# Linear attention: sixteen heads per load and store, Q in 8 KB runs, work still per eight heads

## The chip, the cores and the metric

One core of one Trainium2 chip. The metric is the device time of one execution in microseconds (us). Before: 127.53 us, the median of four runs (126.77 to 127.69). A run more than 1.5% above the fastest of its kernel is called slow and is left out of comparisons. A ratio is the mean time of one kernel's fast runs over that of the other kernel's fast runs of the same rounds, so it is not quite the ratio of the medians quoted; 95% intervals follow it in brackets.

## The reference, cut to what matters

```python
# Q, K, V: (8, 12, 512, 64) float32, so 96 heads of 512 rows
Q_feat = np.maximum(0, Q) + 1
K_feat = np.maximum(0, K) + 1
KV    = np.einsum('bhkd,bhkv->bhdv', K_feat, V)
K_sum = np.sum(K_feat, axis=2)
out   = einsum(Q_feat, KV) / (einsum(Q_feat, K_sum)[..., None] + 1e-10)
```

## The kernel before

Names first: DMA moves data between HBM and the core; DVE is the vector engine, ACT the scalar engine, PE the matrix engine, whose results land in the memory PSUM. A feature is the `max(0, x) + 1` of the reference. The work goes in twelve groups of eight heads. For each group DVE makes the features of K and Q. DVE (three blocks) and ACT (one block) copy V into a block-diagonal form, PE multiplies (`keys_values`), and ACT casts the result. PE transposes the Q features and ACT copies them out of PSUM (`transposes`). PE multiplies again and DVE divides (`output`). The functions that the argument touches, cut (`...` marks what is left out):

```python
def view(t, c):            # partition p holds c successive rows
    return t.flatten_outer_dims().rearrange("(n p c) d -> p n c d", p=P, c=c)
q_dram = view(Q, C2)       # C2 = 16 rows: runs of 4 KB of f32
...
def v_blocks(g):           # DVE takes blocks 0 to 2
    ...
        if b == 3:
            nc.scalar.copy(out=v_blk[g % 2][ps, b], in_=v_raw[ps])
...
def transposes(g):
    qf = qfs.pop(g)
    qt = mid_pool.tile([P, C, P, 2], BF16, name="qt")
    for half in range(2):
        qt_ps = psum_qt.tile([P, C, P], BF16, name="qt_ps")
        for c in range(C):
            nc.tensor.transpose(qt_ps[:, c, :], qf[:, half * C + c, :, :], identity)
        nc.scalar.copy(out=qt[:, :, :, half], in_=qt_ps)   # every 2nd element of qt
...
for g in range(NG - 1):
    k_features(g); v_blocks(g); q_features(g)
    if g:
        transposes(g - 1)
    if g >= 2:
        output(g - 2)
    keys_values(g)
    ...                    # loads and stores
```

## Time and profile before

| | before |
|---|---|
| median time, profiled span | 127.53, 125.8 us |
| ACT busy, of that in the 24 qt copies | 68.0, 29.7 us |
| DVE idle ahead of the output's reciprocals | 4.9 us |
| mean granted clock of PE | 0.839 |

### The profile page before, as it was taken

The numbers are of one execution on the slowest core, as the hardware profiler recorded it, in microseconds if no ns is written. First come the engines' busy times: TensorE is split into PE (matmuls) and PEld (weight loads), VectorE is DVE, ScalarE is ACT, GpSimd is POOL, SyncE is SP. The second block draws the span as 40 slices with busy tenths as digits, with TensorE's granted clock in tenths as the row PEclk, the third lists the DMA queues.
The fourth block names the chain that finished last, engine by engine and source line by source line (L and its number), as shares of the span: only waits on it lengthen the run. The fifth ranks groups of instructions, "written<-read, shape, count | busy, mean of one in ns | idle before, by whom it ended". The sixth has DMA issues, their size and how long they took to land.

```text
span 125.8 us, 2337 instructions
## 1 busy us (share of the span) xinstructions
PE 65.2 (52%) x960; PEld 48.4 (39%) x960; DVE 88.2 (70%) x188; ACT 68.0 (54%) x87; POOL 27.8 (22%) x43
## 2 busy tenths in 40 slices
PE   0005939000059784796918476006978569694500
PEld 0003627000036564574806365004656447472300
DVE  4896280206199799999989990629959999758920
ACT  7832296006700889629892962750087971987000
POOL 6990213000002082023700260212221002020000
PEclk9999999755555999689999999955589976999955
DMA  3999999999999999999999999999999999999991
GB/s 76 341 211 209 210 213 211 210 212 211 212 211 212 211 214 212 210 212 214 253 414 287 209 210 212 213 369 380 209 210 210 211 287 418 418 417 410 403 391 72
DMA packets 13419, 32.13 MB, mean 255 GB/s; under 512 B 608, under 2 KB 608, under 8 KB 13408
## 3 DMA queue, kind: packets, MB, share of 16 engines
q0 software_dynamic: 12048, 28.84, 98.3%
q1 hardware_dynamic: 1360, 3.15, 6.8%
q8 instruction: 7, 0.11, 0.3%
q14 instruction: 4, 0.03, 0.1%
HBM read 37.75 MB, written 12.58 MB: 400 GB/s over the span
## 4 chain that ended last, share of the span: by engine, by line
DMA 40%; DVE 26%; PE 18%; POOL 6%; issue 6%; DVEq 0%; POOLq 0%
DMA q_raw<-in_Q_dram 40%; DVE o_sb L200 15%; PE kva_ps L157 11%; DVE v_all L140 4%; PE qt_ps L176 3%; DVE recip L199 3%; PE o_ps L189 3%; POOL v_raw L99 2%; DVE qf L122 2%; DVE kf L122 2%; POOL q_raw L99 1%; POOL kva_diag L231 1%; POOL k_raw L99 1%; POOL identity masks.py:199 0%; POOL identity masks.py:197 0%
## 5 line engine op out<-in xcount | busy, mean ns | idle before, releaser
L157 PE MATMUL kva_ps<-v_all,kf 128*64 128x320 bf16 x384 | 36.4, 356 | 13.1 <-DVE v_all L140 13.1
L189 PE MATMUL o_ps<-kva_diag,qt 128*64 128x130 bf16 x384 | 19.1, 234 | 40.9 <-DVE o_sb L200 40.4
L200 DVE TENSOR_TENSOR o_sb<-o_ps,recip 128x512 f32<-128x512 f32 x48 | 33.2, 692 | 1.6
L140 DVE COPY v_all<-v_raw 32x2048 bf16<-32x2048 bf16 x36 | 26.5, 736 | 10.9 <-DMA v_raw<-in_V_dram 10.6
L157 PEld LDWEIGHTS <-kf 128*64 128x64 bf16 x384 | 25.3, 133 | 20.9 <-DVE v_all L140 13.3
L189 PEld LDWEIGHTS <-qt 128*64 128x64 bf16 x384 | 12.7, 114 | 46.4 <-DVE o_sb L200 44.6
L138 ACT COPY v_all<-v_raw 32x2048 bf16<-32x2048 bf16 x12 | 22.7, 1894 | 13.3 <-DMA v_raw<-in_V_dram 13.1
L177 ACT COPY qt<-qt_ps 128x1024 bf16<-128x1024 bf16 x24 | 29.7, 1308 | 0.3
L167 ACT CAST kva_diag<-kva_ps 64x256 bf16<-64x256 f32 x24 | 8.9, 371 | 33.3 <-PE kva_ps L157 33.2
L122 DVE TENSOR_SCALAR qf<-q_raw 128x1024 bf16<-128x1024 bf16 x24 | 9.1, 423 | 6.6 <-DMA q_raw<-in_Q_dram 6.5
L99 POOL DMA_DIRECT2D k_raw<-in_K_dram x7 | 5.3, 754 | 38.1 <-DVE kf L122 37.3
L116 POOL DMA_DIRECT2D out_dram<-o_sb x10 | 8.4, 846 | 22.6 <-DVE o_sb L200 16.4
L176 PE MATMUL qt_ps<-identity,qf 128*128 128x128 bf16 x192 | 13.1, 222 | 0.0
L199 DVE RECIPROCAL recip<-o_ps 128x8 f32<-128x8 f32 x48 | 9.6, 199 | 4.9 <-PE o_ps L189 4.8
L122 DVE TENSOR_SCALAR kf<-k_raw 128x1024 bf16<-128x1024 bf16 x22 | 8.7, 437 | 6.0 <-DMA k_raw<-in_K_dram 6.0
L176 PEld LDWEIGHTS <-qf 128*128 128x128 bf16 x192 | 11.0, 99 | 3.3 <-issue 3.0
L99 POOL DMA_DIRECT2D v_raw<-in_V_dram x8 | 6.1, 764 | 18.8 <-ACT v_all L138 10.7
L99 POOL DMA_DIRECT2D q_raw<-in_Q_dram x8 | 5.9, 741 | 4.2 <-DMA q_raw<-in_Q_dram 4.2
L213 DVE MEMSET v_all<- 128x3072 f32 (+1 forms) x2 | 4.4, 2192 | 1.1 <-DVE ones L225 0.7
L168 ACT CAST kva_diag<-kva_ps 64x4 bf16<-64x4 f32 x24 | 4.0, 169 | 0.0
L214 ACT COPY v_all<-zero 128x2048 f32<-128x2048 f32 x2 | 3.7, 1894 | 0.0
L214 ACT ACT_TABLE_LOAD x1 | 1.3, 1283 | 0.7 <-PEq L273 0.7
(12 smaller groups left out, 4.6 us busy)
## 6 DMA issues: line engine op xcount, KB each, us to landing
out_dram<-o_sb POOLq DMA_DIRECT2D x10, 1024.0 KB, 20.2
k_raw<-in_K_dram POOLq DMA_DIRECT2D x4, 1024.0 KB, 18.0
v_raw<-in_V_dram POOLq DMA_DIRECT2D x4, 1024.0 KB, 20.9
q_raw<-in_Q_dram POOLq DMA_DIRECT2D x4, 1024.0 KB, 25.0
v_raw<-in_V_dram POOLq DMA_DIRECT2D x4, 512.0 KB, 17.3
q_raw<-in_Q_dram POOLq DMA_DIRECT2D x4, 512.0 KB, 17.1
out_dram<-o_sb SPq DMA_DIRECT2D x4, 512.0 KB, 5.1
k_raw<-in_K_dram POOLq DMA_DIRECT2D x3, 512.0 KB, 23.3
```

The lines of the kernel that those rows point to most:

```text
L99: nc.gpsimd.dma_start(out=t[:, ms], in_=drams[x][:, 2 * groups[0] : 2 * groups[-1] + 2])
L116: nc.gpsimd.dma_start(out=o_to, in_=o_sb)
L122: nc.vector.tensor_scalar(out=dst, in0=src, scalar1=1.0, scalar2=1.0, op0=ALU.add, op1=ALU.max)
L138: nc.scalar.copy(out=v_blk[g % 2][ps, b], in_=v_raw[ps])
L140: nc.vector.tensor_copy(out=v_blk[g % 2][ps, b], in_=v_raw[ps])
L157: nc.tensor.matmul(kva_ps[64 * n : 64 * n + 64], lhsT=kf[:, c, n, :], rhs=vb[:, :, n, c, :], start=(c == 0), stop=(c == C2 - 1),)
L167: nc.scalar.copy(out=kva[ps, :, n, 0:D], in_=kva_ps[ps, sb : sb + 4, :])
L176: nc.tensor.transpose(qt_ps[:, c, :], qf[:, half * C + c, :, :], identity)
L177: nc.scalar.copy(out=qt[:, :, :, half], in_=qt_ps)
L189: nc.tensor.matmul(ops[c // 4][64 * j : 64 * j + 64, c // 2 % 2, (c % 2) * W : (c % 2) * W + W], lhsT=qt[:, c, 32 * b : 32 * b + 32, :], r ...
L199: nc.vector.reciprocal(out=recip, in_=cells[:, :, :, :, D:D1])
L200: nc.vector.tensor_tensor(out=o_sb[:, h:NP:2, 4 * i : 4 * i + 4].rearrange("p n (b c) d -> p b c n d", b=2), in0=cells[:, :, :, :, 0:D], i ...
```

## The change

Its intent is to move the same bytes in fewer and longer pieces: Q in runs of 8 KB, every bulk load and store 2 MB of f32. Work stays per eight heads, so the buffers for features and PSUM stay as they are. The core of the diff:

```diff
-    q_dram = view(Q, C2)
+    q_dram = view(Q, C4)          # C4 = 32 rows per partition: 8 KB runs
...
 def transposes(g):
-        qt = mid_pool.tile([P, C, P, 2], BF16, name="qt")
+        if g % 2 == 0:
+            qts[g // 2] = mid_pool.tile([P, C, P, 4], BF16, name="qt")
+        qt = qts[g // 2]
...
-            nc.scalar.copy(out=qt[:, :, :, half], in_=qt_ps)
+            nc.scalar.copy(out=qt[:, :, :, g % 2 * 2 + half], in_=qt_ps)
...
 def output(g):
-                        lhsT=qt[:, c, 32 * b : 32 * b + 32, :],
+                        lhsT=qt[:, c, q : q + 16, :],     # q = 16 * (4 * e + b)
...
 for g in range(last):
             if g:
                 transposes(g - 1)
+            if g % 2 == 0:
+                keys_values(g)
             if g >= 2:
                 output(g - 2)
-            keys_values(g)
+            if g % 2:
+                keys_values(g)
...
 # after the loop
-        transposes(last - 1)
         output(last - 2)
-        q_features(last)
         keys_values(last)
+        store(NS - 2)
+        q_features(last - 1)
+        transposes(last - 1)
+        q_features(last)
         transposes(last)
         output(last - 1)
         output(last)
```

One `qt` tile now serves both groups of a pair, and each head's columns come from four copies, two per group; what follows for the order of work is step 3 of the prediction. Not shown in the cut: output buffers fall from 6 to 3 (each of twice the size) and `qt` buffers from 3 to 2.

More of the change, by code (lines that the diff above doesn't have):

```diff
@@ L14 @@
 IN_BUFS = 2
-OUT_BUFS = 6
-LAG = 3
+OUT_BUFS = 3
 @with_exitstack
@@ L44 @@
     C2 = 2 * C
-    NPAIR = B * H * S // (P * C)
-    NP = 4
-    NG = NPAIR // NP
+    C4 = 4 * C
+    NS = B * H // 16
+    NG = 2 * NS
     D1 = D + 1
@@ L62 @@
     feat_pool = ctx.enter_context(tc.tile_pool(name="feat", bufs=2))
-    mid_pool = ctx.enter_context(tc.tile_pool(name="mid", bufs=3))
+    mid_pool = ctx.enter_context(tc.tile_pool(name="mid", bufs=2))
     out_pool = ctx.enter_context(tc.tile_pool(name="out_pool", bufs=OUT_BUFS))
@@ L76 @@
     kva_diag = [const.tile([P, 4, 2, D1], BF16, name=f"kva_diag{i}") for i in range(NV)]
-    drams = dict(k=k_dram, v=v_dram, q=q_dram)
     raw = {}
@@ L83 @@
     outs = {}
-    def own(g):
-        return slice(g % 2 * 2, g % 2 * 2 + 2)
-    def load_first_k():
-        k_raw = head_pool.tile([P, 2, C2, D], FP32, name="k_first")
-        nc.sync.dma_start(out=k_raw, in_=k_dram[:, 0:2])
-        raw["k", 0] = k_raw
-    def load(s, groups, names="kvq"):
-        ms = slice(groups[0] % 2 * 2, groups[-1] % 2 * 2 + 2)
-        for x in names:
-            if (x, "buf", s) not in raw:
-                raw[x, "buf", s] = in_pool.tile([P, 4, C2, D], BF16, name=f"{x}_raw")
-            t = raw[x, "buf", s]
-            nc.gpsimd.dma_start(
-                out=t[:, ms], in_=drams[x][:, 2 * groups[0] : 2 * groups[-1] + 2]
-            )
-            for g in groups:
-                raw[x, g] = t[:, own(g)]
@@ L105, in load_pair, with load_k @@
-    def load_pair(s):
-        if s < NG // 2 - 1:
-            load(s, (2 * s, 2 * s + 1))
-        else:
-            load(s, (2 * s,))
-            load(s, (2 * s + 1,))
-    def store(g):
-        o_sb = outs.pop(g)
-        o_to = o_dram[:, g * NP : g * NP + NP]
-        if g < NG - 2:
-            nc.gpsimd.dma_start(out=o_to, in_=o_sb)
-            return
-        for h in range(2):
-            nc.sync.dma_start(out=o_to[:, h:NP:2], in_=o_sb[:, h:NP:2])
+    def load_k(s, es=(0, 1)):
+        if s == 0 and es == (0,):
+            k_raw = head_pool.tile([P, 2, C2, D], FP32, name="k_first")
+            nc.sync.dma_start(out=k_raw, in_=k_dram[:, 0:4:2])
+            raw["k", 0] = k_raw
+            return
+        k_raw = in_pool.tile([P, 4, C2, D], BF16, name="k_raw")
+        lo, step = es[0], 3 - len(es)
+        nc.gpsimd.dma_start(
+            out=k_raw[:, lo:4:step], in_=k_dram[:, 4 * s + lo : 4 * s + 4 : step]
+        )
+        for e in es:
+            raw["k", 2 * s + e] = k_raw[:, e:4:2]
@@ new lines, in load_v, with load_q @@
+    def load_v(s):
+        v_raw = in_pool.tile([P, 4, C2, D], BF16, name="v_raw")
+        nc.gpsimd.dma_start(out=v_raw, in_=v_dram[:, 4 * s : 4 * s + 4])
+        for e in range(2):
+            raw["v", 2 * s + e] = v_raw[:, e:4:2]
+    def load_q(s):
+        q_raw = in_pool.tile([P, 2, C4, D], BF16, name="q_raw")
+        halves = [slice(e * C2, e * C2 + C2) for e in range(2)]
+        for cs in halves if s == NS - 1 else [slice(0, C4)]:
+            nc.gpsimd.dma_start(out=q_raw[:, :, cs], in_=q_dram[:, 2 * s : 2 * s + 2, cs])
+        for e in range(2):
+            raw["q", 2 * s + e] = q_raw[:, :, halves[e]]
@@ L121, in feature, with store @@
+    def store(s):
+        o_sb = outs.pop(s)
+        o_to = o_dram[:, 8 * s : 8 * s + 8]
+        if s < NS - 1:
+            nc.gpsimd.dma_start(out=o_to, in_=o_sb)
+        else:
+            for i in range(4):
+                nc.sync.dma_start(out=o_to[:, i:8:4], in_=o_sb[:, i:8:4])
     def feature(dst, src):
@@ L176, in transposes @@
                 nc.tensor.transpose(qt_ps[:, c, :], qf[:, half * C + c, :, :], identity)
-            nc.scalar.copy(out=qt[:, :, :, half], in_=qt_ps)
-        qts[g] = qt
+            nc.scalar.copy(out=qt[:, :, :, g % 2 * 2 + half], in_=qt_ps)
     def output(g):
+        s, e = g // 2, g % 2
         kva = kva_diag[g % NV]
-        qt = qts.pop(g)
-        o_sb = out_pool.tile([P, NP, C, D], FP32, name="o_sb")
+        qt = qts[s]
+        if e == 0:
+            outs[s] = out_pool.tile([P, 8, C, D], FP32, name="o_sb")
+        o_sb = outs[s]
         for h in range(2):
@@ L188, in output @@
                     b = 2 * h + j
+                    q = 16 * (4 * e + b)
                     nc.tensor.matmul(
                         ops[c // 4][64 * j : 64 * j + 64, c // 2 % 2, (c % 2) * W : (c % 2) * W + W],
-                        lhsT=qt[:, c, 32 * b : 32 * b + 32, :],
+                        lhsT=qt[:, c, q : q + 16, :],
                         rhs=kva[:, b],
@@ L200, in output @@
                 nc.vector.tensor_tensor(
-                    out=o_sb[:, h:NP:2, 4 * i : 4 * i + 4].rearrange(
+                    out=o_sb[:, 2 * e + h : 8 : 4, 4 * i : 4 * i + 4].rearrange(
                         "p n (b c) d -> p b c n d", b=2
@@ L207, in output @@
                 )
-        outs[g] = o_sb
     def clear(first, split, end):
@@ L219 @@
         nc.gpsimd.memset(zero, 0.0)
-        load_first_k()
-        load(0, (0,), "vq")
-        load(0, (1,))
+        load_k(0, (0,))
+        load_v(0)
+        load_q(0)
+        load_k(0, (1,))
         nc.vector.memset(ones, 0.0)
@@ L231 @@
             nc.gpsimd.memset(t, 0.0)
-        load_pair(1)
+        load_k(1)
+        load_v(1)
+        load_q(1)
         clear(5, 7, 9)
-        for g in range(NG - 1):
+        last = NG - 1
+        for g in range(last):
             k_features(g)
             v_blocks(g)
-            q_features(g)
+            if g < last - 1:
+                q_features(g)
             if g:
                 transposes(g - 1)
+            if g % 2 == 0:
+                keys_values(g)
             if g >= 2:
                 output(g - 2)
-            keys_values(g)
-            if g % 2 and g // 2 + 2 < NG // 2:
-                load_pair(g // 2 + 2)
-            if g >= LAG:
-                store(g - LAG)
-        last = NG - 1
+            if g % 2:
+                keys_values(g)
+                s = g // 2
+                if s + 2 < NS:
+                    load_k(s + 2)
+                    load_v(s + 2)
+                    load_q(s + 2)
+            elif g >= 4:
+                store(g // 2 - 2)
         k_features(last)
         v_blocks(last)
+        output(last - 2)
+        keys_values(last)
+        store(NS - 2)
+        q_features(last - 1)
         transposes(last - 1)
-        output(last - 2)
         q_features(last)
-        keys_values(last)
         transposes(last)
@@ L256 @@
         output(last)
-        for g in range(last - LAG, NG):
-            store(g)
+        store(NS - 1)
 _INS = ['Q', 'K', 'V']
```

## The prediction

> **What bounds the kernel now.** I read the page's shares first, then the slices and queues, then the chain of waits, then the timeline of the last 30 us.
>
> ```profile
> span 125.8 us, 2337 instructions
> ...
> PE 65.2 (52%) x960; PEld 48.4 (39%) x960; DVE 88.2 (70%) x188; ACT 68.0 (54%) x87; POOL 27.8 (22%) x43
> ...
> DVE  4896280206199799999989990629959999758920
> ...
> DMA  3999999999999999999999999999999999999991
> ...
> q0 software_dynamic: 12048, 28.84, 98.3%
> ```
>
> No compute engine is full; the DMA row is at 9 in every slice but the first and last. Loads are cast to bf16, so the page's GB/s count half of what they read. Counting HBM bytes, 37.75 MB read and 12.58 MB written are 50.3 MB. The trace's packets give the pace: loads of 4096 B of f32 run 412 per 4 us over 16 engines, one per 155 ns and engine, 422 GB/s; stores of 4096 B take 157 ns. 50.3 MB at 422 GB/s is 119.3 us of the 125.8. The rest is about 3 us ahead of the first data and 3 us at the ends.
>
> The landing events agree: in mid-kernel each 1 MB bf16 load (2 MB of f32) lands 5.0 us after its predecessor (39.1, 44.1, 49.0, 53.9, 58.9, 63.9), and the last four stores of 512 KB land at 121.1, 122.4, 123.6 and 124.9: a queue that is still draining.
>
> ```profile
> 8.65 25.48 DMA q_raw<-in_Q_dram
> ...
> 59.53 24.54 DMA q_raw<-in_Q_dram
> ```
>
> The chain of waits says it too: its two longest pieces are Q transfers. But between them it runs through DVE and PE, and in the last 40 us DVE is almost full. Compute is a close second. The timeline of the tail:
>
> ```profile
> 99.59 0.76 DVE L122 TENSOR_SCALAR qf<-q_raw 128x1024 bf16<-128x1024 bf16 x2
> ...
> 106.66 0.17 ACT L168 CAST kva_diag<-kva_ps 64x4 bf16<-64x4 f32 x1
> 106.84 0.38 ACT L167 CAST kva_diag<-kva_ps 64x256 bf16<-64x256 f32 x1
> 107.12 0.17 ACT L168 CAST kva_diag<-kva_ps 64x4 bf16<-64x4 f32 x1
> ...
> 107.31 1.89 ACT L138 COPY v_all<-v_raw 32x2048 bf16<-32x2048 bf16 x1
> ...
> 109.23 2.51 ACT L177 COPY qt<-qt_ps 128x1024 bf16<-128x1024 bf16 x2
> ...
> 109.77 2.07 PEld L157 LDWEIGHTS <-kf 128*64 128x64 bf16 x32
> 109.82 2.34 PE L157 MATMUL kva_ps<-v_all,kf 128*64 128x320 bf16 x32
> ...
> 113.55 0.21 DVE L199 RECIPROCAL recip<-o_ps 128x8 f32<-128x8 f32 x1 [1.69 <-PE o_ps L189]
> 113.79 0.69 DVE L200 TENSOR_TENSOR o_sb<-o_ps,recip 128x512 f32<-128x512 f32 x1
> ...
> 115.35 5.41 SPq L119 DMA_DIRECT2D out_dram<-o_sb  x4
> ```
>
> Two things to see. ACT serves in program order: the V copy at 107.31 has had its data since 102.3, but stands behind the kva casts, and those behind keys_values. And output(10) starts at 113.55 although qt(11) is copied only at 113.12 to 115.6: it needs qt(10) alone.
>
> **What the skill says.** "TensorE: Matmul & The Clock Gate", architectural detail: ACT and DVE are strict FIFO. The trace agrees (the V copy, 5 us late). Same page, Part 1: the PE clock is halved when idle and released after about 3.4 us of activity. It agrees: keys_values takes 2.3 us mostly, 3.6 to 4.5 in five of twelve groups. "DMA: Bandwidth & Descriptors", Why small descriptors are slow: about 3 cycles of overhead per packet. It is hardly visible here: stores in 2048 B packets go at 78 ns (512 KB per 1.25 us), so two make 156 ns against 155 for one of 4096 B. Same page, Rules: at least 1 MiB per DMA; the kernel before already has that.
>
> **The change, part by part.**
>
> 1. *Q in 8 KB runs.* 3072 Q packets become 1536 plus the split last load. At 1 ns (above) to 5 ns (the skill's three cycles, rounded up as an estimate) saved for each of some 90 packets per engine: 0.1 to 0.45 us.
>
> 2. *Fewer, larger DMAs.* The queue was never dry, so nothing is gained. Bytes and their order stay: before the last load both kernels place 4 MB of stores. The last load still lands near 104.5.
>
> 3. *The layout's price.* With 32 rows per partition, half of each partition's rows go to the even group and half to the odd. One head's rows thus come from both groups' transposes, and output(even) waits for qt of the odd group too. The order of instructions confirms it: the output of group 10 stands behind all four ACT copies of qt.
>
> For an even group the path is now: out(odd) begins at X on DVE; its last PE tile is written at X+2.0 (two tiles freed at 0.84 us each, 0.4 of matmuls); keys_values(odd) 2.3, X+4.3; four kva casts 0.9, X+5.2; ACT's V copy for the even group 1.9, X+7.1; two qt copies 2.5, X+9.6 (keys_values(even), 2.4 beside them, ends at X+9.5); first tile 0.3: out(even) at X+9.9 to 10.0. DVE meanwhile has 3.2 (output) + 0.8 + 2.3 + 0.8 (K, V, Q) = 7.1, so it idles 2.9 us per sixteen heads. Period: 10 + 3.2 + 3.9 = 17.0 us, against DMA's 15 us of loads, 20 with a 2 MB store.
>
> With landings as before, out(0) starts at 35.9 (PE's slow keys_values(2) from 31.4 to 35.5), out(1) at 42.9, then 59.9, 76.9, 93.9 for the odd ones. Before: 43.0, 57.3, 71.9, 93.4. So DVE falls 5 us behind by group 5 and the wait for Q at 84.1 gives it all back: the middle is nearly free, and the last loads are issued (73.9 to 77) before the queue is dry (about 87).
>
> 4. *The tail.* From X = 93.9: output(7) done 97.1. K (97.9), V lands about 99.2, V blocks 101.4, qt(9) copied 103.6, keys_values(10) 103.8, output(8) 104.0 to 107.2. K and V of 11: 110.3; output(9) to 113.5; Q features 10 and 11 only then, to 115.0. PE: last tile of output(9) 112.3, keys_values(11) 114.7, transposes(10) 115.7. ACT: kva casts to 115.6, then four qt copies at 1.25 = 5.0 (the transposes of 11 fit between them), 120.6. Output(10) begins at 121.0 where before it was 113.8. It and output(11) take 6.5: 127.5 (before 120.4).
>
> The DMA queue is empty by then: stores of 4 and 5, 6 and 7 end near 114, store of 8 and 9 is issued at 113.5 and lands near 122. So the last 512 KB only pays its own latency: the first K load of 1 MB took 5.0 us from issue to landing, less 1.25 for half the bytes is 3.7. Landing 131.2, and 0.9 to the end as before (124.9 to 125.8): span 132.1.
>
> Measured time exceeds the profiled span by 1.75 (127.55 less 125.8): 133.9. Minus 0.4 for Q, plus about 1 for PE's slow clock (1.7 us longer keys_values, weight about a third on two of them on the tail's path): 134.5.
>
> **Rivals.** (a) *DMA still sets the end*: 125.8 less 0.1 to 0.45 of packets, time about 127.2. For it: DMA at 9 everywhere and 2 MB transfers. Against: 120.6 for qt(11) rests on durations that hardly vary (ACT copies 1291 to 1332 ns) and on a fixed order. (b) *8 KB runs are really faster*, for instance 5% on Q (30 us): 126. Against: loads pace at 422 GB/s and show next to no cost per packet. Even then compute would end late. (c) *PE runs slow in most groups*: keys_values(odd) at 4 us adds 1.7 to each period of 17.0 and to both keys_values of the tail: 137 to 139. For it: five slow groups before, gaps of 4 us in PE's new order. Against: from 57 to 77 us it stayed fast with similar gaps. (d) *The tail's idle is smaller*, because DVE is earlier than I have it (V of the last load on time, ACT not blocked): 130 to 131.
>
> **Range and chances.** 134.5, with (d) at 130.5 and (c) at 138.5 as the ends. Faster by over 2% would need (b) and no tail: 0.04. Within 2% is (a), if my reading of the dependency in the tail is wrong somewhere: 0.12. Slower: 0.84.
>
> **What would show it.** Right: a new wait of PE's output, or its weight load, for ACT's qt of about 6 us ahead of output(10), the chain of waits ending in ACT qt and DVE o_sb; DVE idle about 3 us in front of each even output; DMA slices below 9 in the last 15 us; output(11) ending near 127; Q packets of 4096 B (bf16) at twice the old 155 ns pace within 3%; the middle's landings unchanged to 0.5 us. Wrong: DMA slices full to the end with a span under 127 (a or b), Q packets well below 300 ns, or output(10) starting before 117.

## More of the kernel before

From the page of the kernel before come the clock that PE was granted in 40 slices (tenths of full speed) and two groups of instructions. A group's line gives the count, then busy us and mean ns of one, then the idle time of the engine just before them and what ended most of it.

```profile
PEclk9999999755555999689999999955589976999955
...
L177 ACT COPY qt<-qt_ps 128x1024 bf16<-128x1024 bf16 x24 | 29.7, 1308 | 0.3
...
L199 DVE RECIPROCAL recip<-o_ps 128x8 f32<-128x8 f32 x48 | 9.6, 199 | 4.9 <-PE o_ps L189 4.8
```

A qt copy takes 1.3 us. The reciprocal is the first instruction of an output on DVE, so the idle time ahead of it is what outputs cost DVE in waiting: 4.9 us in the whole kernel. The 5s in the clock row are stretches in which PE ran at half speed.

## The result, and the profile after

| | before | after |
|---|---|---|
| median time | 127.53 (126.77 to 127.69) | 156.06 (155.68 to 156.75) |
| profiled span | 125.8 | 154.3 |
| ACT busy, of that qt copies | 68.0, 29.7 | 93.9, 56.5 |
| one qt copy | 1308 ns | 2494 ns |
| mean granted clock of PE | 0.839 | 0.784 |

Four runs of each. The ratio is 1.2257 [1.2186, 1.2328]: 22.6% slower, far beyond the range on record. From the page of the kernel after, the shares, slices, main queue and groups that answer to those shown before:

```profile
span 154.3 us, 2316 instructions
...
PE 81.6 (53%) x960; PEld 60.5 (39%) x960; DVE 89.0 (58%) x188; ACT 93.9 (61%) x87; POOL 21.8 (14%) x34
...
ACT  8413397499840996924996709969179800599000
...
PEclk9999996857955968768995879969599755995555
DMA  5999999999999999999999999999185000770085
...
q0 software_dynamic: 10624, 28.84, 80.3%
...
L178 ACT COPY qt<-qt_ps 128x1024 bf16<-128x1024 bf16 x24 | 56.5, 2494 | 4.9 <-PE qt_ps L177 4.7
L156 PE MATMUL kva_ps<-v_all,kf 128*64 128x320 bf16 x384 | 42.0, 394 | 27.8 <-DVE v_all L139 20.1
...
L203 DVE RECIPROCAL recip<-o_ps 128x8 f32<-128x8 f32 x48 | 9.6, 199 | 41.4 <-PE o_ps L193 41.4
```

First, DVE has hardly more work than before (89.0 against 88.2 us), but now waits 41.4 us ahead of its outputs. Second, ACT has gained 26 us of work, all of it in the qt copies: same shape, same count, nearly twice the time. Third, the DMA row is full for three quarters of the span and then falls to 0: the queue runs dry in the tail. Fourth, PE's clock is lower: the means of 0.784 and 0.839, with half speed and full speed as the only two levels in these traces, amount to 67 us at half speed against 40. A rival can be struck out here: no wait in this trace is put down to a store's landing or a `qt` buffer still in use, so the fewer buffers are not the cause.

The chain of waits of the kernel after shows one round of the loop (columns: start us, duration us, then engine, tile, line and count):

```profile
65.67 0.69 DVE o_sb L204
66.50 0.70 DVE o_sb L204
67.25 0.65 PE o_ps L193 x8
67.90 3.52 PE kva_ps L156 x32
72.36 1.89 ACT v_all L137
74.27 4.73 ACT qt L178 x2
79.75 0.69 DVE o_sb L204
...
86.81 0.69 DVE o_sb L204
```

This is the very loop of the prediction's step 3: the odd output's last tiles, `keys_values(5)`, ACT's casts and V copy, two qt copies, then the even output, and the next odd output at 86.8. Set beside the prediction's terms:

| term, us | predicted | measured |
|---|---|---|
| odd output's start to the last PE tile written | 2.0 | 2.4 |
| keys_values(odd) | 2.3 | 3.5 |
| kva casts | 0.9 | 0.9 |
| V copy | 1.9 | 1.9 |
| two qt copies | 2.5 | 4.7 |
| even output's first tile | 0.3 | 0.5 |
| DVE: even output, K, V, Q | 7.1 | 7.1 |
| period | 17.0 | 21.1 |

The column is the difference of successive starts in the chain and the trace, from 65.5 to 86.6. Every term has the place that was foreseen. Two of them are far off: the copies (+2.2) and `keys_values` (+1.2). The tail repeats it. From the same view:

```profile
129.44 3.47 PE kva_ps L156 x32
133.85 6.95 ACT qt L178 x3
140.81 2.27 ACTq L298
143.12 0.66 PE o_ps L193 x8
144.05 0.69 DVE o_sb L204
```

The step that the chain calls "ACTq 2.27" is the fourth qt copy. The timeline shows it as one row of four copies, 133.85 to 143.06. The prediction had this wait ("four qt copies at 1.25 = 5.0"). It lasts 9.2 us.

### The profile page after: what moved, and what is told of

The parts are those of the page before. It is cut to its first block, busy times and chain, and to the rows that moved or that the text cites. A ratio compares the mean times of both kernels' runs of the same rounds, so it can differ in the third digit from the quotient of the medians.

```text
span 154.3 us, 2316 instructions
## 1 busy us (share of the span) xinstructions
PE 81.6 (53%) x960; PEld 60.5 (39%) x960; DVE 89.0 (58%) x188; ACT 93.9 (61%) x87; POOL 21.8 (14%) x34
## 4 chain that ended last, share of the span: by engine, by line
DVE 32%; ACT 28%; PE 15%; DMA 15%; POOL 3%; issue 3%; ACTq 1%; POOLq 0%
ACT qt L178 20%; DVE o_sb L204 17%; DMA v_raw<-in_V_dram 15%; PE kva_ps L156 11%; DVE v_all L139 7%; ACT v_all L137 6%; PE o_ps L193 4%; DVE recip L203 4%; DVE kf L121 2%; DVE qf L121 2%; ACT kva_diag L166 2%; ACTq L298 1%; POOL kva_diag L235 1%; POOL k_raw L91 1%; ACT kva_diag L167 1%
## 5 line engine op out<-in xcount | busy, mean ns | idle before, releaser
L178 ACT COPY qt<-qt_ps 128x1024 bf16<-128x1024 bf16 x24 | 56.5, 2494 | 4.9 <-PE qt_ps L177 4.7
L156 PE MATMUL kva_ps<-v_all,kf 128*64 128x320 bf16 x384 | 42.0, 394 | 27.8 <-DVE v_all L139 20.1
L156 PEld LDWEIGHTS <-kf 128*64 128x64 bf16 x384 | 30.0, 147 | 36.6 <-DVE v_all L139 20.5
L193 PE MATMUL o_ps<-kva_diag,qt 128*64 128x130 bf16 x384 | 24.7, 279 | 36.2 <-DVE o_sb L204 24.6
L193 PEld LDWEIGHTS <-qt 128*64 128x64 bf16 x384 | 16.4, 140 | 45.0 <-DVE o_sb L204 30.5
L203 DVE RECIPROCAL recip<-o_ps 128x8 f32<-128x8 f32 x48 | 9.6, 199 | 41.4 <-PE o_ps L193 41.4
L177 PE MATMUL qt_ps<-identity,qf 128*128 128x128 bf16 x192 | 17.0, 258 | 4.1 <-ACT qt L178 4.1
L177 PEld LDWEIGHTS <-qf 128*128 128x128 bf16 x192 | 14.5, 118 | 7.3 <-issue 7.2
L91 POOL DMA_DIRECT2D k_raw<-in_K_dram x6 | 4.5, 754 | 56.5 <-DVE kf L121 56.5
L115 POOL DMA_DIRECT2D out_dram<-o_sb x5 | 5.6, 1115 | 45.4 <-DVE o_sb L204 45.4
L99 POOL DMA_DIRECT2D v_raw<-in_V_dram x6 | 4.6, 768 | 7.4 <-issue 3.9
L107 POOL DMA_DIRECT2D q_raw<-in_Q_dram x7 | 4.9, 709 | 0.0
```

The lines of the kernel that those rows point to most:

```text
L91: nc.gpsimd.dma_start(out=k_raw[:, lo:4:step], in_=k_dram[:, 4 * s + lo : 4 * s + 4 : step])
L115: nc.gpsimd.dma_start(out=o_to, in_=o_sb)
L156: nc.tensor.matmul(kva_ps[64 * n : 64 * n + 64], lhsT=kf[:, c, n, :], rhs=vb[:, :, n, c, :], start=(c == 0), stop=(c == C2 - 1),)
L178: nc.scalar.copy(out=qt[:, :, :, g % 2 * 2 + half], in_=qt_ps)
L193: nc.tensor.matmul(ops[c // 4][64 * j : 64 * j + 64, c // 2 % 2, (c % 2) * W : (c % 2) * W + W], lhsT=qt[:, c, q : q + 16, :], rhs=kva[:, ...
L203: nc.vector.reciprocal(out=recip, in_=cells[:, :, :, :, D:D1])
```

## The experiments

The first theory was that the slow copies are the cause, because they now write 8 bytes apart. Its rival was that PE's clock is: with longer waits PE is granted half its clock more often, `keys_values` gets longer, and the copies lie beside other work. A third thought was that the tail alone could be mended. Runs marked "wrong" compute a wrong result to isolate a cost; all others were correct.

**Copies with a step of 4 bytes, in the order of the kernel after** (wrong: neighbouring rows instead of interleaved ones).

```diff
-            qts[g // 2] = mid_pool.tile([P, C, P, 4], BF16, name="qt")
+            qts[g // 2] = mid_pool.tile([P, C, 2, P, 2], BF16, name="qt")
...
-            nc.scalar.copy(out=qt[:, :, :, g % 2 * 2 + half], in_=qt_ps)
+            nc.scalar.copy(out=qt[:, :, g % 2, :, half], in_=qt_ps)
```

> The changed kernel with one thing undone: the ACT copies of qt write every second bf16 (a step of 4 bytes, as in the kernel before) instead of every fourth (8 bytes); which half of a tile the output matmuls read is then wrong, so the result is wrong on purpose, but counts, sizes, order and the wait of output(even) for both groups' qt are kept. Theory (the copy's write step is the cause): copies fall from 2494 to about 1308 ns and the time to my own blind sum, 132 to 138 us. Rival (the order of instructions, the later stores and PE's slow clock are the cause): copies may fall, the time stays above 148 us.

Measured: 145.93 us (145.58 to 148.79, five runs), ratio 1.1427 [1.1358, 1.1495]. The clock row, `keys_values` and the qt group on its page:

```profile
PEclk9999995955985777965859955999857996589555
...
L156 PE MATMUL kva_ps<-v_all,kf 128*64 128x320 bf16 x384 | 46.4, 425 | 28.0 <-DVE v_all L139 20.6
...
L178 ACT COPY qt<-qt_ps 128x1024 bf16<-128x1024 bf16 x24 | 29.6, 1314 | 1.5 <-PE qt_ps L177 1.3
```

The copies are back at 1.31 us, so the write step is what slows them. They are worth 10.1 us (156.06 to 145.93). But 11.4 us remain above the 134.5 of the prediction (the blind sum from here on), where the copies' theory alone wanted nearly none: the time lies between the two expectations. The rest fits the clock rival: in this trace `keys_values` takes 4.0 to 4.5 us in ten of twelve groups, and in the chain two even ones (4.0 us each) now end later than the two copies beside them (2.5).

**Copies with a step of 8 bytes in the kernel before** (wrong).

```diff
-        qt = mid_pool.tile([P, C, P, 2], BF16, name="qt")
+        qt = mid_pool.tile([P, C, P, 4], BF16, name="qt")
...
-                        lhsT=qt[:, c, 32 * b : 32 * b + 32, :],
+                        lhsT=qt[:, c, 64 * (b // 2) : 64 * (b // 2) + 64, b % 2],
```

> The kernel before with only this added: qt has four slots per column, of which the ACT copies fill two, so they write with a step of 8 bytes; the output's weights are read with the same step (wrong result on purpose). Theory: copies rise from 1308 to about 2490 ns with everything else as it was, ACT's busy time from 68 to about 96 us, and the time to 129 to 137 us, since in this order an output waits only for copies of a group earlier. Rival (something else in the changed kernel makes its copies slow, such as PE's writes or waits beside them): copies stay near 1308 ns and the time within 1% of before.

Measured: 128.75 us (128.56 to 128.98, four runs), ratio 1.0094 [1.0054, 1.0135]. From its page:

```profile
DMA  3999999999999999999999999999999999999954
...
L177 ACT COPY qt<-qt_ps 128x1024 bf16<-128x1024 bf16 x24 | 56.9, 2505 | 0.3
```

The copies double here as well, in the old order and with nothing else changed but the step at which the output's weights are read. But the time hardly moves: just under the range expected. The same 27 us of ACT work cost 1.2 us where DMA stays at 9, and about 10 where the copies stand in the loop. So what counts is where the copies stand, not how busy ACT is.

**The cost of the step by itself** (wrong on purpose; one look): the kernel before with the steps 1, 2, 3, 4, 6 and 8 in successive groups (and 4 output buffers instead of 6).

```diff
+STEPS = (1, 2, 3, 4, 6, 8, 1, 2, 3, 4, 6, 8)
...
+            qt = qt[:, 0 : C * P * st].rearrange("d (c p k) -> d c p k", k=st, p=P)
```

> A measurement, in the kernel before: the twelve groups' qt copies write with steps of 1, 2, 3, 4, 6, 8, 1, 2, 3, 4, 6, 8 elements of bf16 (wrong result on purpose). Step 2 should give 1.31 us and step 4 2.49. If the cost follows the bytes spanned, step 1 gives about 1.05 (ACT's floor), step 3 about 1.9, step 6 3.7, step 8 4.9. If it is a step from one level to another, 6 and 8 give 2.5 as 4 does. If the skill's 16-byte lines (two hits per line at full rate) held for these writes, steps up to 4 would cost the same and 6 and 8 more.

| step, bf16 elements (bytes) | one copy of 1024 elements per partition, ns |
|---|---|
| 1 (2) | 1015 |
| 2 (4) | 1292 to 1319 |
| 3 (6) | 1866 to 1936 |
| 4 (8) | 2422 to 2578 |
| 6 (12) | 3617 to 3797 |
| 8 (16) | 4761 to 5062 |

From step 2 on the time goes in proportion to the step, about 0.6 ns per element and unit of step (2500 / 1024 / 4); at step 1 it stops at a floor of 1015 ns. The run took 142.3 us, against 127.5 for the kernel before on the same chip.

**The tail in another order**: the Q features and transposes of the last two groups ahead of their K and V work.

```diff
+        q_features(last - 1)
+        transposes(last - 1)
+        q_features(last)
+        transposes(last)
         k_features(last)
         v_blocks(last)
         output(last - 2)
         keys_values(last)
         store(NS - 2)
-        q_features(last - 1)
-        transposes(last - 1)
-        q_features(last)
-        transposes(last)
```

> The changed kernel, correct, its copies left slow, only the tail reordered: Q features and transposes of groups 10 and 11 go ahead of K, V and output(9). Theory (slow copies in every pair of groups, and four of them exposed in the tail): only the tail's part comes back, 156 to 147 to 151 us. Rival (the tail's order is most of the loss): 140 us or less.

Measured: 154.93 us (154.34 to 155.67, four runs), ratio 1.2149 [1.2086, 1.2211]: about 1 us better, if at all (its interval overlaps that of the kernel after), and a miss. Its timeline says why:

```profile
126.38 9.27 ACT L178 COPY qt<-qt_ps 128x1024 bf16<-128x1024 bf16 x4 [4.76 <-PE qt_ps L177]
...
135.67 1.89 ACT L137 COPY v_all<-v_raw 32x2048 bf16<-32x2048 bf16 x1
137.62 4.48 PE L156 MATMUL kva_ps<-v_all,kf 128*64 128x320 bf16 x32 [2.38 <-ACT v_all L137]
...
142.57 0.21 DVE L203 RECIPROCAL recip<-o_ps 128x8 f32<-128x8 f32 x1 [6.35 <-PE o_ps L193]
```

The four copies now run 7.5 us earlier, but ACT's V copy of group 11 stands behind them. `keys_values(11)` waits for that, at half clock, and the next output starts only 1.2 us earlier than before (142.8 against 144.0). The wait has changed its name.

**Filling PE's idle time**, to test the clock: 24 spare matmuls ahead of the second half of odd outputs and 14 ahead of even `keys_values`, into unused PSUM.

```diff
+    def fill(g, n):
+        ...
+        for _ in range(n):
+            nc.tensor.matmul(t, lhsT=identity, rhs=identity, start=True, stop=True)
...
+                fill(g, 14)
                 keys_values(g)
...
-                output(g - 2)
+                output(g - 2, 24 if g % 2 else 0)
```

With the 4-byte step (wrong, as its base):

> The kernel with copies at a step of 4 bytes (wrong result on purpose, 145.9 us) and, added, filler matmuls of 128 columns that nothing reads: 24 in the idle time of PE before the second half of each odd output, 14 before each even keys_values, so that PE's clock is not halved. Theory (what is left over my blind sum is PE's slow clock in both keys_values of a pair): keys_values falls from 4.0 to 2.3 to 2.7 us and the time to 134 to 139. Rival (the order of the waits, with PE's clock a bystander): keys_values falls and the time stays above 143.

Measured: 141.15 us (139.68 to 143.01, four runs); the two fast runs, 139.68 and 140.28, give 1.0996 [1.0927, 1.1065]. From its page:

```profile
L165 PE MATMUL kva_ps<-v_all,kf 128*64 128x320 bf16 x384 | 38.0, 367 | 18.6 <-DVE v_all L139 14.2
```

`keys_values` is busy for 38.0 us instead of 46.4, and the mean granted clock is 0.878 where the same kernel without fillers had 0.787. More work on PE makes the kernel some 6 us shorter: that part goes with the clock. Of the 5.5 us that remain above 134.5, some may be clock still: after the first 40 us its record has half speed from 63 to 67, 80 to 84, 111 to 121 us and from 128 to the end, the last two in the tail. The rest this run doesn't explain.

With the slow copies, in the kernel after itself (here 20 and 14 fillers, and 18 more ahead of even outputs):

> The changed kernel, correct, copies left slow at 2.5 us, with the same filler matmuls (20, 14, and 18 more between the even keys_values and the even output). If the two causes simply add, keys_values at 2.3 us takes 1.4 to 2 us from each of four or five pairs: 156 to 146 to 150. If the slow copies cover the slow clock, it stays above 153.

Measured: 155.27 us (151.63 to 156.03, four runs), of which only 151.63 (clock 0.856) counts as fast, between the two expectations. One run gives no interval; the verdict is unclear. Its trace shows the clock's part beside slow copies: `keys_values` takes 2.3 us for groups 5, 7 and 9, and output(9) starts at 122.6 instead of 127.2.

**The same layout with fast copies.** Each copy writes the two halves of a group side by side, in pairs of elements.

```diff
+            qt_ps = psum_qt.tile([P, 2, 4, P], BF16, name="qt_ps")
...
-            nc.scalar.copy(out=qt[:, :, :, g % 2 * 2 + half], in_=qt_ps)
+            nc.scalar.copy(
+                out=qt[:, cs : cs + 4, :, k : k + 2],
+                in_=qt_ps.rearrange("d h c p -> d c p h"),
+            )
```

> The changed kernel with a correct remedy for the copies: the two transposes that belong to neighbouring slots lie in one PSUM tile, and each ACT copy takes four columns of both, so that it writes pairs of bf16 over half the bytes (4096 instead of 8192 per copy of 1024 elements). If the cost follows the bytes spanned by the writes, copies take 1.3 us and the time is that of the step of 4 bytes, 143 to 149. If every jump of the write or the PSUM read costs instead, copies stay at 2 us or more and the time above 150.

Measured: 143.77 us (140.76 to 147.75, four runs): 140.76 and 141.46 fast, 146.08 and 147.75 slow; no interval was given.

```profile
L182 ACT COPY qt<-qt_ps 128x1024 bf16<-128x1024 bf16 x24 | 23.0, 1017 | 1.1 <-PE qt_ps L179 0.9
```

The pairs still lie 8 bytes apart, yet the copy takes 1017 ns, the floor, less than in the kernel before and than the 1.3 us expected: the bytes spanned are not what is paid for. The result is correct, and the fast runs are 15 us below the kernel after.

With the fillers added:

> The paired copies and the filler matmuls together, correct. Theory (both terms undone leave my blind sum): 133 to 139 us. Rival (something else remains): above 142.

Measured: 135.74 us (134.67 to 138.81, four runs, three fast), ratio 1.0635 [1.0570, 1.0700]. Clock and queue of this run, from the view of the cores and from the page:

```profile
core 0: 133.5 us, clock 0.901
```
```profile
DMA  4999999999999999999999999999999998079484
```

With fast copies and most of the slow clock gone, the change costs about what the blind sum said: 135.7 against 134.5. That is partly luck: these copies are 0.2 us each faster than the sum's, and the loop still lags in the middle and catches up later. Odd outputs start at 43.1, 61.6, 80.0, 96.7 and 112.8, where the prediction had 42.9, 59.9, 76.9, 93.9 and 110.3.

**Other orders.** The question was now whether an order exists that hides the loop. Four kernels built on the paired copies: m1 has `keys_values(odd)` between the halves of the odd output; m2 has the tail reordered too; m3 is m2 with Q in two loads of 4 KB runs; m4 is m2 with 14 fillers ahead of each `keys_values`.

```diff
 def output(g, between=None):
         for h in range(2):
+            if h and between is not None:
+                keys_values(between)
```

> Paired copies (correct, 141 us fast) with one move in the loop: keys_values of an odd group runs between the halves of the odd output on PE instead of after it, which takes it, its casts and ACT's next V copy off the way between an odd output and the next even one. Theory (the new wait of output(even) for the odd group's qt, a loop through PE and ACT, is the third term, some 3 us of DVE idleness a pair): the loop becomes DMA's, out(9) starts 8 to 10 us earlier, the tail stays: 131 to 137 us. Rival (the loop is set by PE's or DVE's own work): above 139.

Measured: 143.71 us (139.90 to 144.98, four runs), one run fast, 139.9, against 141.1 for the mean of the paired copies' fast runs: a miss. The profile kept is of a slow run. In that of m3, a fast run with the same order in the loop, the odd outputs take 3.5 to 5.2 us on DVE instead of 3.2, so DVE loses part of what `keys_values` gains.

The tail of m2 takes the Q work and transposes of the last groups first and stores in parts:

```diff
+        q_features(last)
+        transposes(last - 1)
         k_features(last)
         v_blocks(last)
-        output(last - 2)
-        keys_values(last)
-        store(NS - 2)
-        q_features(last - 1)
-        transposes(last - 1)
-        q_features(last)
         transposes(last)
+        store(NS - 2, 0)
+        output(last - 2, last)
+        store(NS - 2, 1)
```

> The same with the tail reordered (Q features of groups 10 and 11 and the transposes ahead of output(9), keys_values(11) inside output(9)) and the last store but one in two 1 MB parts. Theory: the layout with 8 KB runs then costs nothing and DMA's 50.3 MB set the end again: 126 to 130 us, between 1% under and 2% over before. Rival: some loss stays with the layout whatever the order, above 132.

Measured: 138.93 us (134.66 to 142.10, six runs), one fast, 134.66: a miss.

```diff
-        for cs in halves if s == NS - 1 else [slice(0, C4)]:
+        for cs in halves:
             nc.gpsimd.dma_start(out=q_raw[:, :, cs], in_=q_dram[:, 2 * s : 2 * s + 2, cs])
```

> The same kernel with every Q load cut into two loads of 4 KB runs, as the kernel before has them: the 8 KB runs by themselves. My step 1 says 0.1 to 0.45 us more than the run with 8 KB runs; the intent of the change (longer runs are cheaper) would need 1 us or more.

Measured: 136.03 us (134.78 to 138.68, six runs, four fast), ratio 1.0642 [1.0576, 1.0707]. The fast runs, 134.78 to 136.17, can't be told apart from the one fast run of m2; n3 below repeats the comparison with six fast runs on each side.

```diff
+        for _ in range(14 if g % 2 else 14):
+            nc.tensor.matmul(spare, lhsT=identity, rhs=identity, start=True, stop=True)
```

> Reordered loop and tail with 14 filler matmuls ahead of each keys_values, to keep PE's clock up. If DMA sets the end without them, no change within 1%; if slow keys_values still delay outputs in the tail, 1 to 3 us less.

Measured: 132.19 us (131.36 to 134.79, four runs, three fast), ratio 1.0350 [1.0286, 1.0414]: the best of all sixteen-head kernels, still 3.5% behind the kernel before.

**The odd transposes early** (n1), inside the odd output, with `keys_values` behind the outputs and a fourth `kva` buffer. By my count this order had no loop left that exceeds DMA's pace.

```diff
+            if g % 2:
                 transposes(g - 1)
+                if g > 1:
+                    output(g - 2, [(transposes, g)])
...
+            elif g:
                 output(g - 2)
+            keys_values(g)
```

> Paired copies, and a new order (correct): the odd group's transposes run inside the odd output of the same round, one round earlier than in the changed kernel, so qt is whole before the even output wants it; keys_values stands behind each output; in the tail K, V and Q of groups 10 and 11 and keys_values(11) go ahead of output(8); the last store but one in parts. If the loss was order and not layout: 125.5 to 128.5 us, within 1% of before. If the layout itself costs: above 130.

Measured: 138.84 us (137.44 to 139.36, six fast runs), ratio 1.0857 [1.0810, 1.0904]: a miss by ten. PE's waits in this trace (us in total, times, longest):

```profile
PE o_ps L206 <- DVE o_sb L217: 22.9, 19, 7.4
...
PE qt_ps L182 <- ACT qt L185: 10.8, 8, 2.4
```

Two PSUM buffers serve the transposes. The odd group's transposes wait for ACT to empty them, and the second half of the output waits behind the transposes in PE's order: an odd output takes 6.0 us on DVE instead of 3.2.

With 14 fillers ahead of each `keys_values`:

> The same with 14 filler matmuls ahead of each keys_values. If PE's clock is off the path in this order, no change within 1%; if it still matters, 1 to 3 us less than without.

Measured: 140.18 us (136.54 to 141.12, four runs), one fast: unclear.

The same with Q in two loads of 4 KB runs (n3; the edit is that of m3):

> The new order with every Q load in two of 4 KB runs. With the queues at the bound the 8 KB runs are worth what packets say: 0.1 to 0.45 us, so this is 0 to 0.5 us slower than with 8 KB runs. The change's intent would want over 1 us.

Measured: 135.0 us (133.79 to 135.67, six fast runs), ratio 1.0556 [1.0508, 1.0604]: 3.8 us faster than with 8 KB runs, the intervals far apart, where up to 0.5 us slower was expected. In the traces 2 MB of Q take 4.9 to 5.0 us either way, but the first half can be used when it has landed. For the second pair of groups that is at 32.4 us, where the whole load lands at 34.5 (32.3 in m3 and 34.6 in m2 above). The first output starts at 33.4 instead of 35.6, the odd ones at 40.8, 58.1, 75.2 and 92.3 instead of 43.6, 61.0, 78.3 and 95.6: a lead won at the start and kept, as both run at about 17.3 us a pair.

With the slow copies in this order:

> The new order with the changed kernel's copies at a step of 8 bytes (2.5 us, correct). If the new order leaves room, as the kernel before did (128.75 us with such copies), 128 to 133 us; if slow copies cost 10 us in any order, 136 or more.

Measured: 156.03 us (154.10 to 156.31, four fast runs), ratio 1.2167 [1.2096, 1.2238]. Set against the paired copies' 138.84, the 8-byte step costs 17 us in another order of the same work. It is not a quirk of the one order.

## Why the prediction was wrong, point by point

**Right: what bounds the kernel before, and the mechanism.** Compute was called a close second. The loop (step 3), the dependency of even outputs on the odd group, the four copies ahead of output(10) and the empty queue at the end (step 4) all stand in the trace in the place given. Slower was given 0.84.

**Right: steps 1 and 2.** Four Q loads in mid-kernel land 4.85 to 4.94 us after their predecessors, against 4.92 to 5.00 before: a mean gain of 0.06 us, some 0.3 for the five whole loads, within the 0.1 to 0.45 foreseen. The packets' own records promise more (324 ns for 4096 B against twice 173 before), but they overlap: 16 per engine in 4.89 us are 306 ns each. So the landings decide. Landings match those of before to 0.5 us up to the Q load at 84.0. Of the kernel before, only the last four stores (512 KB each) are short of the 1 MiB that the prediction says it already has. And larger DMAs bought nothing: split Q loads were faster in n3.

**Wrong: the term "two qt copies 2.5" of step 3 and its twin "four qt copies at 1.25 = 5.0" of step 4.** I took the duration of the copy before for a copy whose destination had changed. The diff shows the change in two characters (`P, 2` to `P, 4`), and rival (a) was even argued away with "ACT copies 1291 to 1332 ns". Measured: 4.7 a pair, 9.2 for four. On the path this is 2.2 us in each of four periods plus 4.2 in the tail, 13.1 us before rounding.

**Wrong: the term "keys_values(odd) 2.3".** Measured on the path, from the last output tile to the first cast, 4.2, 3.5, 3.2 and 3.2 in the loop and 3.5 in the tail: 6.1 us more, for which the prediction had set aside "about 1". Rival (c) named this cost, but gave 137 to 139, with the copies at their old speed. The argument against it ("from 57 to 77 us it stayed fast with similar gaps") carried one stretch of the old trace over to a new one, in which PE is without matmuls for 73 us (154.3 less 81.6) instead of 61.

Together 19.2 of the 23.1 us by which the last output ends late (150.6 against 127.5). Of the other 3.9, 1.0 is there when output(1) begins (43.9 against 42.9), and two slow copies (4.8 us from 31.1) are on the chain ahead of it. The rest is in small terms, five times each: some 0.4 in the odd output's first term (2.4 for 2.0) and 0.2 in the even output's first tile (0.5 for 0.3).

The experiments bear the two sizes out only roughly, because they are not independent. Taking the slow copies away saved 10.1, not 13.1, while `keys_values` grew to 4.0 us and more and for two even groups came onto the chain; fillers then saved some 6 more. That longer waits lower the clock, which lengthens `keys_values`, which lengthens the waits, is my reading of this; shown are the two effects, not the circle.

**Step 3's "the middle is nearly free" fell with its size.** At 17.0 us per pair the lag was to be given back at the wait for Q at 84.1. At 21 us it was not: output(7) began at 107.4, predicted 93.9. The loads were on time (the last landed at 105.4, predicted 104.5), but output(7) came 13.5 us late, so no wait for data was left to take the loss up, and it went straight into the end.

Open: why a write of single elements goes with the step while pairs 8 bytes apart run at the floor; and whether some order brings the sixteen-head layout back to 127. Seven kernels with fast copies in other orders or with split loads or fillers (m1 to m4, n1 to n3) did not; the best was 132.2.

## What to carry to other kernels

When a diff changes the layout of a tile, price every instruction that reads or writes it anew; a duration from the old profile holds for the old access pattern only. A cost that sits in slack (1.2 us here) can be worth ten or more once a new dependency puts it into a loop, so ask of each instruction on the new path what it takes now, the clock of PE included. And before buying longer DMA runs, check whether the pace per byte leaves anything for longer runs to gain: here 8 KB bought less than 0.1 us a load, and waiting for the whole load cost more.

## What the Trainium skill lacked or had wrong

- "SBUF — State Buffer", section "Door 1: The DMA port swizzle", the note on cachelines: it says that accesses within a 16-byte line go at full bandwidth with two or more hits, and that one can stride 8 bf16 for free. For ACT's writes the runs differ: steps of 2, 3, 4 and 8 bf16 took 1.31, 1.9, 2.5 and 4.9 us against 1.015 at step 1, and 2.5 us is at two hits per line. The measurement decides; pairs of bf16 (4 bytes) 8 bytes apart took 1.017.
- "ScalarE: Activation LUTs", section "What ACT_TABLE_LOAD costs": it gives 186 ns + 0.833 N with immediates, an estimate of 1039 ns for N = 1024. It agrees with 1015 at step 1, but the page has no word on the step of the destination, which made the same copy 4.9 us at step 8.
- No page says what single-element strided writes cost on ACT, nor that pairing them takes the cost away (2494 to 1017 ns in the same layout).
